# Fox/mLSTM decoder step on one core: the second place of gathered values given up ahead of the seventh MLP step's products, and five stores and one copy at the attention's two ends on other engines

## The chip, the core and the metric

The kernel runs on one core of one Trainium2 chip. The core has TensorE (PE, matrix products), VectorE (DVE), ScalarE (ACT), GpSimd (POOL) and SyncE (SP), which run beside each other and wait for each other by semaphores, and 16 DMA engines, which SP, ACT and POOL start. The metric is the device time of one launch in microseconds (us), the median of several runs; less is better.

## The reference

One step of a decoder layer. A prompt of 2048 tokens and 8 sequences of 8 new tokens (each with 8192 cached positions in pages) go through one input projection, two kinds of heads, one output projection with layer norm, and a squared-ReLU MLP with layer norm. Cut to the prompt's part:

```python
z = x @ w_in                       # fox q, k, v, f; mLSTM q/k, v, i, f, o
# 8 heads of 64: causal attention with forget gates
s = q_i @ k.T * Dh ** -0.5 + L_i[..., :, None] - L[:, :, None, :]
fox = softmax(where(k_pos <= q_pos, s, -inf)) @ v
# 4 heads of 128: matrix memory, chunk by chunk
C_new = g_state * C + einsum('bhs,bshd,bshe->bhde', w_key, k, v)
n_new = g_state * n + einsum('bhs,bshd->bhd', w_key, k)
mix = concat([fox, norm(h) * mlstm_norm_w * sigmoid(o)]) @ w_o
x1  = layer_norm(DN_ALPHA * x + mix)
y   = layer_norm(DN_ALPHA * x1 + square(relu(x1 @ w1)) @ w2)
```

The samples' fox heads attend to `cache_k` and `cache_v` by the page table. C and n after the last chunk are outputs (`C_prompt`, `n_prompt`), as are k and v (`k_prompt`, `v_prompt`).

## The kernel before

Four stages follow one another. The first (0 to 869.5 us) makes the input projections and the matrix memory; the second (to 1309.5, `phase_b`) is the prompt's attention; the third (to 1540, `phase_o`) the output projection and the first layer norm; the fourth (`phase_c`) the MLP. Products in float32 are made of parts: an operand x is split into a rounded part xh (`split_hi`, L153, on ACT) and the rest xl (`split_lo`, L156, on DVE), and `mm3` (L162 to L164) adds three products wh·xh, wl·xh and wh·xl in this order of lines.

Beside all of it the samples' attention runs as a generator, from which the stages take a step now and then. It gathers pages of `cache_v` by POOL's indirect DMAs (L1838) into one of two places: `vt`, which is always there, and a second one, `vx["more"]`, which is lent by the stage that runs and taken back by setting it to `None`. Their products are sO (L1862).

In the attention, `units` lists 64 pairs (head h, block g of 256 queries). `scores` (L981, L982) multiplies the queries' parts qh and ql by the keys' ks, and DVE adds the forget values nl (L989; for the diagonal block nd, which POOL makes of nl and a mask at L974) and takes the maximum. `values` makes the softmax on ACT (L1010), transposes S by TensorE to pt (L1026), copies it to PT (L1029, L1031), multiplies by the values vn to po (L1036), copies one half of po to ot (L1041) and adds the other (L1043). After every fourth block `finish` turns the sums to a row of factors through DRAM (drl, rl), multiplies on POOL (L1061) and stores to `dmix` (L1062). The first head loads nl (L932), vn (L933), the keys kn (L938) and the queries qn (L956) as it goes; the first kn and qn were loaded earlier (L226). `phase_o` loads `dmix` as xr, splits it to mh and ml and multiplies it with the parts of w_o (wh, wl) to pw.

The matrix memory ends with the stores of C (L749) and n (L752, its copy nn), and `turn_out` transposes the last chunk's output (L644, mm), copies it (L646, ot) and stores it to `dmix` (L647).

The code order is the order of creation; a scheduler then fixes each engine's order when the kernel is built. Eight semaphores (DMAHW0 to 7) are given in turn to the DMAs which SP and ACT start, eight others (DMASW0 to 7) to POOL's. A DMA waits until the one that had its semaphore before has landed; each engine takes its instructions strictly in order, so what stands behind such a wait waits too.

Of the kernel before, what the change touches and what calls it, by code (L numbers as in the profile page):

```python
# [25 lines left out]
S = 2048  # L26
# [26 lines left out]
def body(ctx, tc, I, O, stages):  # L53
    nc = tc.nc
    V, A, G, T, SY = nc.vector, nc.scalar, nc.gpsimd, nc.tensor, nc.sync
# [12 lines left out]
    dmix = drm.tile([8, 128, TOT], F32, name="dmix")  # L68
# [40 lines left out]
    vx = dict(more=None, live=[], next=0, of={})  # L109
# [512 lines left out]
    dmv = dmix.rearrange("j p t -> p j t")  # L622
# [3 lines left out]
    def norm_out(hh, np_, og, tok0, eng=None):  # L626

        st = pm.tile([128, 4, 6], F32, name="st6", bufs=2)
        mv = pm.tile([128, 4, 2], F32, name="mv2", bufs=2)
        for h in range(4):  # L630
            V.bn_stats(st[:np_, h], hh[:, h])
            V.bn_aggr(mv[:np_, h], st[:np_, h])
        r = pm.tile([128, 2, 4], F32, name="r4", bufs=2)
        V.tensor_scalar(r[:np_, 0], mv[:np_, :, 1], EPS, None, op0=OP.add)
        G.tensor_tensor(r[:np_, 1], r[:np_, 0], nhalf[:np_, 0:4], op=OP.pow)
        for h in range(4):
            V.tensor_scalar(hh[:, h], hh[:, h], mv[:np_, h, 0:1], r[:np_, 1, h:h + 1], op0=OP.subtract, op1=OP.mult)
        hf = hh.rearrange("p h e -> p (h e)")
        (eng or G).tensor_tensor(hf, hf, og, op=OP.mult)

        def turn():
            po = ppm.tile([128, 4, 128], F32, name="mm", tag="mm", bufs=2)
            for h in range(4):
                T.transpose(po[:, h, :np_], hh[:, h], ident[:np_, :np_])  # L644
            ot = pm.tile([128, 4, 128], F32, name="ot", bufs=1)
            A.copy(ot[:, :, :np_], po[:, :, :np_])  # L646
            SY.dma_start(dmv[:, 4:8, tok0:tok0 + np_], ot[:, :, :np_])  # L647
        mst["turn"] = turn

    def turn_out():  # L650
# [28 lines left out]
    def m_block(bi):  # L679
# [10 lines left out]
        for c in range(bi * 4, bi * 4 + 4):  # L690
            Cs = mst["C"]
# [30 lines left out]
            for p in range(2):  # L722
                yield 1
                pn = ppm.tile([128, 2, 129], F32, name="mn", tag="mm", bufs=2)
                for i in range(2):
                    h = 2 * p + i
# [5 lines left out]
            for p in range(2):  # L732
# [4 lines left out]
                for i in range(2):  # L737
                    h = 2 * p + i
# [7 lines left out]
        if bi < 3:  # L746
            return
        Cs = mst["C"]
        SY.dma_start(O["C_prompt"][0, 0].rearrange("h d e -> d h e"), Cs[:, :, 0:128])  # L749
        nn = pm.tile([128, 4], F32, name="nn", tag="sm", bufs=1)  # L750
        V.tensor_copy(nn, Cs[:, :, 128])
        SY.dma_start(O["n_prompt"], nn)  # L752
        yield 1
        turn_out()

# [148 lines left out]
    def phase_b():  # L904
# [95 lines left out]
        def values(z, g, sc):  # L1000
# [37 lines left out]
            if g % 4 == 0:  # L1038
                z["ot"] = pb.tile([64, 1024], F32, name="ot", bufs=2)
            od = z["ot"][:, (g % 4) * 256:(g % 4) * 256 + 256]  # L1040
            A.copy(od, po[0:64])  # L1041
            q0 = 128 if g == 0 else 0
            V.tensor_tensor(od[:, q0:], od[:, q0:], po[64:128, q0:], op=OP.add)  # L1043
            if g % 4 == 3:
# [2 lines left out]
        def finish(z, half):  # L1047

            h, ls, ot = z["h"], z["ls"], z["ot"]
            lr = pb.tile([128, 32], F32, name="lr", bufs=2)  # L1050
            V.reciprocal(lr, ls)
            lt = pb.tile([128, 32], F32, name="lt", bufs=2)
            V.transpose(lt, lr)
            o = half * 1024
            for a in range(4):
                SY.dma_start(drl[h, o:o + 1024].rearrange("(t a q) -> a t q", a=4, q=32)[a], lt[a * 32 + half * 8:a * 32 + half * 8 + 8])
            for q in range(2):
                rl = pb.tile([64, 512], F32, name="rl", bufs=2)
                SY.dma_start(rl, dap(drl, h * S + o + q * 512, [[0, 64], [1, 512]]))
                s = slice(q * 512, (q + 1) * 512)  # L1060
                G.tensor_tensor(ot[:, s], ot[:, s], rl, op=OP.mult)  # L1061
                SY.dma_start(dmix[h // 2, (h % 2) * 64:(h % 2) * 64 + 64, o + q * 512:o + q * 512 + 512], ot[:, s])  # L1062

        kns = [pb.tile([128, 512], F32, name="kn", bufs=3)]
        homes = {}
# [224 lines left out]
    def phase_c():  # L1290
# [51 lines left out]
        for ci, blk in enumerate(CB):  # L1342
# [201 lines left out]
            hidden(0, 1)  # L1544
            for p in range(8):
                pre = []
                if p == 7 and ci == 3:
                    plain(p)
                    break
                if p < 7:  # L1550
                    hidden(p + 1, 0, lambda: pre.append(ahead(p, *order[:2])))
                else:
                    pre.append(ahead(p, *order[:2]))
                if p == 6:
                    vx["more"] = None
                with ExitStack() as es_:
                    if "normed" in C:
                        es_.enter_context(tc.issue_after(C.pop("normed").ins))
                    output(p, pre[0], begun if p == 7 and ci < 3 else None)
                if p == 7 and ci < 3:  # L1560
                    vx["more"] = landing
                    C["w1"] = w1_pieces(0)
                    C["gb"] = vecs(2)
                    later = [normed(t, ys[t], C["gb"]) for t in blk]
                if p == 6 and ci < 3:
                    take_back()
                    begun = [x1_load(t) for t in CB[ci + 1][:2]]
                if p == 6 and ci == 2:
                    while acc[1] is not None:
                        tick(100.0)  # L1570
                if p < 7:
                    hidden(p + 1, 1, {2: sampled, 3: early}.get(ci) if p == 6 else None)
# [437 lines left out]
```

## Time and profile before

| | us |
|---|---|
| three runs | 3205.98, 3209.95, 3212.35 (median 3209.95) |
| profiled execution | 3212.34 (span 3210.6) |
| granted TensorE clock, mean of the span | 0.989 |
| TensorE busy, 0 to 869.5 | 847.87 of 869.5 |
| TensorE busy, 1309.5 to 1540 | 224.41 of 230.5 |

Times in the profile run from the span's start. In a timeline row the first number is when a group of instructions starts, the second how long it takes, then engine, line, operation, out<-in, shapes and count; brackets hold the idle time of the engine just before it and what ended it. SPq, ACTq and POOLq rows are an engine's DMA issues, and their time is that of issuing, not of the transfer. Ends of matrix products are modelled, so neighbours can overlap a little.

### The profile page before, as it was taken

The page shows a single profiled execution, that of the slowest core. Times are in us where ns is not written, and L with a number is a line of the kernel's source. Part 1 is how long each engine was busy: PE and PEld are TensorE (multiplying, and loading weights), DVE is VectorE, ACT ScalarE, POOL GpSimd, SP SyncE. Part 2 cuts the span into 40 slices and gives each one's busy share as a digit, 9 for nine tenths or more (in the row PEclk, how much of TensorE's full clock was granted, in tenths as well). Part 3 has the DMA queues.
Part 4 walks back from the last instruction along what each step waited for, and adds up shares of the span by engine and source line. Part 5 has one row for each costly group of instructions (what it writes and reads, how often), then busy time and mean ns, then how long its engine had stood idle before and what let it go on. Part 6 is the DMA issues. An engine that isn't in the chain of part 4 may idle for free. (4 is left out here: it accounts for less than half of the span.)

```text
span 3210.6 us, 55049 instructions
## 1 busy us (share of the span) xinstructions
PE 3115.6 (97%) x20445; PEld 2475.3 (77%) x20445; DVE 2080.9 (65%) x5046; ACT 1442.2 (45%) x2654; POOL 902.6 (28%) x973
## 2 busy tenths in 40 slices
PE   8999999999899999999999999999999999899998
PEld 8997797888767667777677777777767777698886
DVE  6957556465488788534557568556675665766667
ACT  3343343333277777412444445343444444344442
POOL 0121223423333333376333323334333111000000
PEclk9999999999999999999999999999999999999999
DMA  5565766866777865687887869878879866643231
GB/s 190 156 216 179 253 210 211 295 238 228 238 241 189 204 170 138 223 295 257 300 289 269 308 234 322 319 260 307 292 260 340 288 209 204 211 165 131 98 126 63
DMA packets 325075, 732.67 MB, mean 228 GB/s; under 512 B 63592, under 2 KB 161384, under 8 KB 323912
## 3 DMA queue, kind: packets, MB, share of 16 engines
q1 hardware_dynamic: 237672, 414.67, 39.8%
q0 software_dynamic: 83520, 304.12, 27.3%
q10 hardware_dynamic: 3616, 10.36, 0.9%
q8 instruction: 162, 2.65, 0.3%
q14 instruction: 105, 0.86, 0.1%
HBM read 676.20 MB, written 86.38 MB: 238 GB/s over the span
## 5 line engine op out<-in xcount | busy, mean ns | idle before, releaser
L156 DVE TENSOR_TENSOR wl<-wr,wh 128x1024 fp32r<-128x1024 f32 x300 | 365.9, 1223 | 244.0 <-ACT wh L153 204.8
L153 ACT ACTIVATE wh<-wr 128x1024 fp32r<-128x1024 f32 x300 | 315.3, 1055 | 332.0 <-PE py L164 123.7
L162 PE MATMUL ph<-x1h,wh 128*128 128x512 f32 (+1 forms) x1280 | 455.4, 356 | 0.0
L163 PE MATMUL ph<-x1l,wh 128*128 128x512 f32 (+1 forms) x1280 | 453.7, 355 | 0.2 <-DVE x1l L156 0.2
L164 PE MATMUL ph<-x1h,wl 128*128 128x512 f32 (+1 forms) x1280 | 451.7, 355 | 0.2
L1727 POOL DMA_INDIRECT kT<-cache_k,idxK x256 | 277.0, 1082 | 551.9 <-PE sQ L1750 483.2
L162 PE MATMUL py<-wh,hh 128*128 128x512 f32 x900 | 358.9, 403 | 10.1 <-issue 3.6
L163 PE MATMUL py<-wl,hh 128*128 128x512 f32 x900 | 354.5, 395 | 0.2 <-issue 0.2
L164 PE MATMUL py<-wh,hl 128*128 128x512 f32 x900 | 351.8, 395 | 0.4 <-DVE hl L156 0.4
L1376 DVE TENSOR_TENSOR y<-y,py 128x512 f32<-128x512 f32 x410 | 277.2, 683 | 108.4 <-PE py L164 83.0
L1838 POOL DMA_INDIRECT vt<-cache_v,idxV x164 | 178.9, 1091 | 401.4 <-PE sO L1862 341.5
L162 PEld LDWEIGHTS ph<-x1h,wh 128*128 128x128 f32 x1280 | 241.4, 189 | 40.6 <-issue 8.2
L164 PEld LDWEIGHTS ph<-x1h,wl 128*128 128x128 f32 x1280 | 240.8, 189 | 36.5 <-issue 3.7
L163 PEld LDWEIGHTS ph<-x1l,wh 128*128 128x128 f32 x1280 | 241.5, 189 | 34.9 <-issue 3.7
L162 PE MATMUL pm<-whi,xh 128*128 128x256 f32 (+2 forms) x816 | 238.2, 292 | 8.0 <-ACT whi L153 7.9
L163 PE MATMUL pm<-wlo,xh 128*128 128x256 f32 (+2 forms) x816 | 233.9, 287 | 1.0 <-DVE wlo L156 0.6
L164 PE MATMUL pm<-whi,xl 128*128 128x256 f32 (+2 forms) x816 | 234.1, 287 | 0.0
L162 PE MATMUL pm<-xh,whi 128*128 128x512 f32 (+2 forms) x640 | 230.5, 360 | 0.0
L164 PE MATMUL pm<-xh,wlo 128*128 128x512 f32 (+2 forms) x640 | 227.4, 355 | 0.0
L163 PE MATMUL pm<-xl,whi 128*128 128x512 f32 (+2 forms) x640 | 226.8, 354 | 0.0
L162 PEld LDWEIGHTS py<-wh,hh 128*128 128x128 f32 x900 | 169.3, 189 | 66.1 <-issue 25.8
L164 PEld LDWEIGHTS py<-wh,hl 128*128 128x128 f32 x900 | 170.7, 190 | 40.3 <-issue 2.3
(364 smaller groups left out, 6545.2 us busy)
## 6 DMA issues: line engine op xcount, KB each, us to landing
wr<-w SPq DMA_DIRECT2D x200, 512.0 KB
wra<-w_in SPq DMA_DIRECT2D x104, 512.0 KB
wr<-dw SPq DMA_DIRECT2D x96, 512.0 KB
dw<-w POOLq DMA_DIRECT2D x48, 512.0 KB
Rb<-dR SPq DMA_DIRECT2D x128, 128.0 KB
kT<-dw SPq DMA_DIRECT2D x28, 512.0 KB
kT<-w SPq DMA_DIRECT2D x25, 512.0 KB
xn<-xp_t SPq DMA_DIRECT2D x16, 512.0 KB
```

Of the source, the lines that this page charges most:

```text
L153: last["ACT"] = A.activation(dst, src, AF.Copy, scale=scale)
L156: r = (eng or V).tensor_tensor(dst, src, hi.bitcast(F32), op=OP.subtract)
L162: T.matmul(ps, wh, xh, start=first, stop=False, skip_group_check=shared)
L163: T.matmul(ps, wh, xl, start=False, stop=False, skip_group_check=shared)
L164: last["PE"] = T.matmul(ps, wl, xh, start=False, stop=stop, skip_group_check=shared)
L1376: V.tensor_tensor(y, y, ps, op=op)
L1727: G.indirect_dma_start(out=piece(n), out_offset=None, in_=ck, in_offset=IO(ap=idxK[:, b, j // 2, j % 2:j % 2 + 1], axis=0))
L1838: vx["last"] = G.indirect_dma_start(out=vt.rearrange("p f c -> p (f c)"), out_offset=None, in_=cv, in_offset=IO(ap=idxV[:, b, (kt % 4) * 4 ...
```

## The change

The stores of C_prompt, n_prompt and the last mLSTM chunk's output are started by ACT instead of SP. At the attention's end, the last unit's copy of po is made by DVE instead of ACT, and the last two stores to `dmix` are started by POOL instead of SP. In the MLP, `vx["more"] = None` at p == 6 is set before the call of `hidden(7, 0)` instead of after it. Lines behind L1041 have a number higher by 3 in the changed kernel. `turn_out`, `finish` and `values` are called as before.

```diff
--- before.py
+++ after.py
@@ -644,7 +644,7 @@
                 T.transpose(po[:, h, :np_], hh[:, h], ident[:np_, :np_])
             ot = pm.tile([128, 4, 128], F32, name="ot", bufs=1)
             A.copy(ot[:, :, :np_], po[:, :, :np_])
-            SY.dma_start(dmv[:, 4:8, tok0:tok0 + np_], ot[:, :, :np_])
+            (A if tok0 == S - 128 else SY).dma_start(dmv[:, 4:8, tok0:tok0 + np_], ot[:, :, :np_])
         mst["turn"] = turn
 
     def turn_out():
@@ -746,10 +746,10 @@
         if bi < 3:
             return
         Cs = mst["C"]
-        SY.dma_start(O["C_prompt"][0, 0].rearrange("h d e -> d h e"), Cs[:, :, 0:128])
+        A.dma_start(O["C_prompt"][0, 0].rearrange("h d e -> d h e"), Cs[:, :, 0:128])
         nn = pm.tile([128, 4], F32, name="nn", tag="sm", bufs=1)
         V.tensor_copy(nn, Cs[:, :, 128])
-        SY.dma_start(O["n_prompt"], nn)
+        A.dma_start(O["n_prompt"], nn)
         yield 1
         turn_out()
 
@@ -1038,7 +1038,10 @@
             if g % 4 == 0:
                 z["ot"] = pb.tile([64, 1024], F32, name="ot", bufs=2)
             od = z["ot"][:, (g % 4) * 256:(g % 4) * 256 + 256]
-            A.copy(od, po[0:64])
+            if (z["h"], g) == units[-1]:
+                V.tensor_copy(od, po[0:64])
+            else:
+                A.copy(od, po[0:64])
             q0 = 128 if g == 0 else 0
             V.tensor_tensor(od[:, q0:], od[:, q0:], po[64:128, q0:], op=OP.add)
             if g % 4 == 3:
@@ -1059,7 +1062,7 @@
                 SY.dma_start(rl, dap(drl, h * S + o + q * 512, [[0, 64], [1, 512]]))
                 s = slice(q * 512, (q + 1) * 512)
                 G.tensor_tensor(ot[:, s], ot[:, s], rl, op=OP.mult)
-                SY.dma_start(dmix[h // 2, (h % 2) * 64:(h % 2) * 64 + 64, o + q * 512:o + q * 512 + 512], ot[:, s])
+                (G if (h, half) == (7, 1) else SY).dma_start(dmix[h // 2, (h % 2) * 64:(h % 2) * 64 + 64, o + q * 512:o + q * 512 + 512], ot[:, s])
 
         kns = [pb.tile([128, 512], F32, name="kn", bufs=3)]
         homes = {}
@@ -1544,6 +1547,8 @@
             hidden(0, 1)
             for p in range(8):
                 pre = []
+                if p == 6:
+                    vx["more"] = None
                 if p == 7 and ci == 3:
                     plain(p)
                     break
@@ -1551,8 +1556,6 @@
                     hidden(p + 1, 0, lambda: pre.append(ahead(p, *order[:2])))
                 else:
                     pre.append(ahead(p, *order[:2]))
-                if p == 6:
-                    vx["more"] = None
                 with ExitStack() as es_:
                     if "normed" in C:
                         es_.enter_context(tc.issue_after(C.pop("normed").ins))
```

How the instructions stand, at three places. First SP at the attention's start, from the last Rb loads of the samples' attention to the first queries. The bracket names the semaphore whose former DMA has to have landed (DMAHW), or the engine waited for. Before:

```order
L1734 DMA Rb<-dR 128x1x256 [waits DMAHW5_49]
L749 DMA C_prompt<-Cs 128x4x128 [waits DMAHW7_49,DVE_49]
L752 DMA n_prompt<-nn 128x4 [waits DMAHW0_49,DVE_49]
L647 DMA dmix<-ot 128x4x128 [waits DMAHW1_49,Activation_49]
L932 DMA nl_10000<-dnl 128x512 [waits DMAHW2_49]
L933 DMA vn_9999<-v_prompt 128x4x64 [waits DMAHW3_49]
L938 DMA kn<-k_prompt 64x512 [waits DMAHW4_49]
L938 DMA kn<-k_prompt 64x512 [waits DMAHW5_49]
L932 DMA nl_10000<-dnl 128x512 [waits DMAHW6_49]
L933 DMA vn_9999<-v_prompt 128x4x64 [waits DMAHW7_49]
L956 DMA qn<-dq 64x256 [waits DMAHW0_49,PE_49]
```

Now, SP and then ACT:

```order
L1737 DMA Rb<-dR 128x1x256 [waits DMAHW5_49]
L932 DMA nl_10000<-dnl 128x512 [waits DMAHW1_49]
L933 DMA vn_9999<-v_prompt 128x4x64 [waits DMAHW3_49]
L938 DMA kn<-k_prompt 64x512 [waits DMAHW4_49]
L938 DMA kn<-k_prompt 64x512 [waits DMAHW5_49]
L932 DMA nl_10000<-dnl 128x512 [waits DMAHW6_49]
L933 DMA vn_9999<-v_prompt 128x4x64 [waits DMAHW7_49]
L956 DMA qn<-dq 64x256 [waits DMAHW0_49,PE_49]
```

```order
L604 DMA v_prompt<-st 128x256 [waits DMAHW6_49,Activation_49]
L749 DMA C_prompt<-Cs 128x4x128 [waits DMAHW7_49,DVE_49]
L752 DMA n_prompt<-nn 128x4 [waits DMAHW0_49,DVE_49]
L646 COPY ot<-mm 128x512 [waits DMAHW1_49,PE_49]
L153 ACTIVATE qh<-qn_9739 128x256 [waits DMAHW5_49]
L153 ACTIVATE ks_10001<-kn_9738 128x512
L647 DMA dmix<-ot 128x4x128 [waits DMAHW2_49,Activation_49]
L1010 ACTIVATE S,lp<-S,mx 128x128 [waits DVE_49]
```

The first nl is no longer behind the three stores. The second nl, the vn behind it and the first qn wait on DMAHW6, 7 and 0, and the DMAs which had these before them are v_prompt, C_prompt and n_prompt, in both kernels; in the changed one they are in ACT's queue.

Second, TensorE at the same time: the first unit of the attention. Before:

```order
L644 MATMUL mm<-ident,hh 128x128 x4
L981 MATMUL pS<-ks_10001,qh 128x256
L982 MATMUL pS<-ks_10001,ql 128x256
L981 MATMUL pS<-ks_10001,qh 128x256
L982 MATMUL pS<-ks_10001,ql 128x256
L1026 MATMUL pt<-ident,S 128x128 x3
L981 MATMUL pS<-ks_10001,qh 128x384
L981 MATMUL pS<-ks_10001,qh 128x512
L1036 MATMUL po<-PT,vn_9999 64x256
L1036 MATMUL po<-PT,vn_9999 64x128
L982 MATMUL pS<-ks_10001,ql 128x384
```

Now:

```order
L1026 MATMUL pt<-ident,S 128x128 x3
L1036 MATMUL po<-PT,vn_9999 64x256
L1036 MATMUL po<-PT,vn_9999 64x128
L981 MATMUL pS<-ks_10001,qh 128x384
L981 MATMUL pS<-ks_10001,qh 128x512
L982 MATMUL pS<-ks_10001,ql 128x384
```

The first unit's po products stand ahead of the second unit's first scores. A few products and transposes of the next units of the first head changed places in the same way; from there on TensorE's order is the same to the end.

Third, the attention's end: ACT before, with the last unit's copy ahead of the output projection's splits, and DVE now.

```order
L1041 COPY ot<-po 64x256
L1029 COPY PT<-pt 128x4x128 x3
L1029 COPY PT<-pt 128x3x128
L1029 COPY PT<-pt 128x4x128
L1041 COPY ot<-po 64x256
L153 ACTIVATE mh<-xr 128x1024
L153 ACTIVATE wh<-wr 128x1024 x4
```

```order
L1031 COPY PT<-pt 128x4x128
L1042 COPY ot<-po 64x256
L1046 TENSOR_TENSOR ot<-ot,po 64x256
L84 MEMSET pad_5x 128x1
L156 TENSOR_TENSOR ml<-xr,mh 128x1024
L156 TENSOR_TENSOR wl<-wr,wh 128x1024 x4
```

The second copy of ot has left ACT, where mh and wh now follow the copies of PT, and stands on DVE between a copy of PT and the addition. Everything behind stands as before.

## The prediction

> **What bounds the kernel now.** I read the page first, then busy time by stage, then TensorE's waits, and only then the two places which the diff touches, engine by engine. From the page:
>
> ```profile
> span 3210.6 us, 55049 instructions
> PE 3115.6 (97%) x20445; PEld 2475.3 (77%) x20445; DVE 2080.9 (65%) x5046; ACT 1442.2 (45%) x2654; POOL 902.6 (28%) x973
> ```
>
> TensorE (PE) is busy for 3115.6 of 3210.6 us, so 95.0 us of idle time is all that an edit which leaves its work alone can win. By stage (columns: stretch, its length, then busy time of PE, PEld, DVE, ACT, POOL, the granted PE clock, DMA share, GB/s):
>
> ```profile
> 869.50:1309.50 440.00, 416.33 (x2880) 295.80 (x2880) 348.88 (x1373) 327.95 (x765) 151.74 (x237) 0.98 0.68 180
> 1540.00:3210.60 1670.60, 1626.95 (x9869) 1263.97 (x9867) 1089.19 (x1838) 727.81 (x1123) 380.85 (x365) 0.99 0.68 238
> ```
>
> The attention leaves 23.7 us idle, the MLP 43.7 us. TensorE's waits, by what they wait for (total, times, longest):
>
> ```profile
> PE sO L1862 <- DMA vt<-cache_v,idxV: 18.3, 6, 6.2
> PE pt L1026 <- ACT S L1010: 10.5, 3, 7.4
> ```
>
> The first is the waiting for gathered values, which the MLP edit is about. The second contains one stall of 7.4 us, and it stands exactly where the stores are moved, at the attention's start:
>
> ```profile
> 869.54 0.58 PE L981 MATMUL pS<-ks,qh 128*128 128x256 f32 x1 [2.23 <-DVE ks L156]
> ...
> 870.35 0.41 PE L982 MATMUL pS<-ks,ql 128*128 128x256 f32 x1
> 878.18 0.48 PE L1026 MATMUL pt<-ident,S 128*128 128x128 f32 x1 [7.42 <-ACT S L1010]
> ...
> 879.65 1.11 PE L981 MATMUL pS<-ks,qh 128*128 128x384 f32 x2
> 880.70 1.12 PE L1036 MATMUL po<-PT,vn 128*64 128x256 f32 x4
> 881.74 1.12 PE L982 MATMUL pS<-ks,ql 128*128 128x384 f32 x2
> ```
>
> Four score products end at 870.76 (878.18 less 7.42). Then TensorE waits for the first softmax. What that softmax waits for is seen on GpSimd (POOL) and on SyncE's queue:
>
> ```profile
> 876.53 1.69 POOL L974 TENSOR_TENSOR nd<-nl,dmask 128x128 f32<-128x128 f32 x4 [8.70 <-DMA nl<-dnl]
> ```
>
> ```profile
> 862.69 1.18 SPq L1734 DMA_DIRECT2D Rb<-dR  x2
> 867.14 0.39 SPq L749 DMA_DIRECT2D C_prompt<-Cs  x1
> 867.62 0.72 SPq L752 DMA_DIRECT2D n_prompt<-nn  x1
> 868.43 0.63 SPq L647 DMA_DIRECT2D dmix<-ot  x1
> 869.12 0.68 SPq L932 DMA_DIRECT2D nl<-dnl  x1
> ...
> 870.38 1.25 SPq L938 DMA_DIRECT2D kn<-k_prompt  x2
> 874.23 0.34 SPq L932 DMA_DIRECT2D nl<-dnl  x1
> 874.76 0.37 SPq L933 DMA_DIRECT2D vn<-v_prompt  x1
> 875.23 2.38 SPq L956 DMA_DIRECT2D qn<-dq  x4
> ```
>
> The forget values nl leave SP at 869.12, behind three stores, and are used at 876.53. SP then stands still until 874.23, and only afterwards come the next queries (875.23). Why it stands:
>
> ```profile
> SPq L932 <- DMA v_prompt<-st: 2.6, 1, 2.6
> SPq L933 <- DMA C_prompt<-Cs: 0.2, 1, 0.2
> ```
>
> Eight semaphores are handed out in turn to the DMAs of SP and ACT, so a load waits for the store that had its semaphore eight DMAs ago. The second nl waits for a v_prompt store, the vn behind it for C_prompt.
>
> **The change, part by part: the attention's start.** The stores of C_prompt, n_prompt and the last dmix go to ScalarE's (ACT) queue. SP can issue the first nl when the Rb pair is out, at 862.69 + 1.18 = 863.87, instead of 869.12: 5.25 us earlier. By the trip that it has now (869.12 to 876.53, 7.41 us) its use would be at about 871.3, and the first unit of attention (softmax, transposes pt, products po) would run in what is now idle time.
>
> The second step is the next unit's queries. Their loads stand behind the second nl and vn, and by the instruction rows of the changed kernel these still wait for the same stores: nl for v_prompt, vn for C_prompt, qn for n_prompt. None of them leaves earlier than now:
>
> ```profile
> 865.94 0.34 ACTq L604 DMA_DIRECT2D v_prompt<-st  x1
> 879.19 0.96 ACT L153 ACTIVATE qh<-qn 128x256 fp32r<-128x256 f32 x2
> ```
>
> v_prompt is issued by ACT at 865.94, before and after the change, and C_prompt can't go ahead of 867.14, when its data is ready. So if the landings stay, qn leaves at 875.23 as now, and the second unit's scores stay near 879.65. Most of the stall is then only split up, not removed. Two things remain. The first unit's po products now stand ahead of these scores, where before they stood behind the first two of them: 881.74 less 880.70, 1.04 us, moves into the idle time. And the queries' trip, 875.23 to 879.19, is 3.96 us now, with the first nl, vn and kn still under way. A load at the attention's end takes less:
>
> ```profile
> 1304.27 1.11 SPq L1059 DMA_DIRECT2D rl<-drl  x2
> 1307.28 1.26 POOL L1061 TENSOR_TENSOR ot<-ot,rl 64x512 f32<-64x512 f32 x1 [23.25 <-DMA rl<-drl]
> ```
>
> That is 3.01 us, 0.95 less. Together 2.0 us, which I take. The bounds are 5.25 us of gain (everything from the first nl on moves with it) and a loss of 7.4 us (the stores land later by the whole trip of the load that now goes ahead of them). I take a value near nothing because the rows name v_prompt and C_prompt, and neither is issued earlier.
>
> On ACT the two issues stand ahead of the ot copy and of the splits qh and ks: 0.39 + 0.72 = 1.11 us later first scores. Queued behind them is everything of ACT; TensorE waits for it, but its scores would end at 871.9 and nl is due at 871.3, so this costs nothing as long as the softmax waits for loads. If that cover goes, it costs 1.11 us. The third store's issue (0.63 us) lies in ACT's wait for the softmax.
>
> The scheduler also put some products and transposes of the next units in another order. The nearest row for what such a place can cost is
>
> ```profile
> 905.12 0.66 PE L1026 MATMUL pt<-ident,S 128*128 128x128 f32 x4 [2.59 <-ACT S L1010]
> ```
>
> so it lies between -2.6 (this wait vanishes) and +2.6 us (one more like it). I take 0, as the same work is done and no row favours a side.
>
> **The attention's end.** There one copy goes from ACT to VectorE (DVE), and two stores from SP to POOL:
>
> ```profile
> 1305.88 3.67 PE L1036 MATMUL po<-PT,vn 128*64 128x256 f32 x32
> 1311.92 0.50 PE L162 MATMUL pw<-wh,mh 128*128 128x512 f32 x1 [2.38 <-ACT wh L153]
> 1314.05 0.80 PE L163 MATMUL pw<-wl,mh 128*128 128x512 f32 x1 [1.62 <-DVE wl L156]
> ```
>
> ```profile
> 1309.60 0.37 ACT L1041 COPY ot<-po 64x256 f32<-64x256 f32 x1 [3.03 <-PE po L1036]
> ```
>
> ```profile
> 1310.00 0.42 DVE L1043 TENSOR_TENSOR ot<-ot,po 64x256 f32<-64x256 f32 x1 [4.30 <-ACT ot L1041]
> 1310.96 1.90 DVE L156 TENSOR_TENSOR ml<-xr,mh 128x1024 fp32r<-128x1024 f32 x1 [0.53 <-ACT mh L153]
> ```
>
> Now ACT waits 3.03 us for the last po before it may begin the output projection's splits mh and wh. Without the copy they run ahead, and the 2.38 us wait for wh goes. But the next product needs wl, which DVE makes after ml, and DVE still has copy and add first. By ACT's 0.37 the copy would end at 1309.97 and the add at 1310.39; ml starts near 1310.45 instead of 1310.96, and wl and the product at 1314.05 move with it: 0.5 us. The 2.38 us becomes a longer wait at the second product. The bounds are 1.0 us of gain (the hand-off and the short memset both hidden) and 0.4 us of loss (a copy twice as long as ACT's).
>
> On POOL a store's issue costs
>
> ```profile
> L1140 POOL DMA_DIRECT2D dw<-w x48 | 35.5, 793 | 0.1
> ```
>
> 0.79 us, so two delay what is behind them, the gathers of vx, by 1.6 us. Their first use on TensorE is
>
> ```profile
> 1341.63 1.05 PE L1862 MATMUL sO<-vx,PTs 128*32 128x256 f32 x16
> ```
>
> some 30 us after the stage's start, so I cost this at nothing; with that cover gone it would be 1.6 us. SP is relieved of the same two, but its next loads still wait for POOL's last product.
>
> **The MLP.** The two lines which move one assignment ahead of a call change no row: every engine has the same instructions in the same order, with the same waits, and each wait has the same producer. So no gather is issued between the old place of the assignment and the new one. I take 0.
>
> **The sum** is -2.0 - 0.5 = -2.5 us. The profiled execution took 3212.34 us, its span 3210.6 and 1.74 around it, so it would take 3209.8. It lies 2.39 us above the median of the three runs shown, 3209.95, so against the median the forecast is 3207.4 us.
>
> **The rivals.**
>
> First, the whole train moves (B). If v_prompt and C_prompt land sooner, as fewer loads are issued in one burst with them, the later loads follow the first, and the stall shrinks by 5.25 us. The clock then gains as well:
>
> ```profile
> 872.00:880.00 8.00, 1.29 (x4) 0.82 (x5) 2.14 (x12) 2.25 (x8) 2.14 (x5) 0.50 0.83 204
> 880.00:890.00 10.00, 9.02 (x43) 5.55 (x42) 8.64 (x41) 5.61 (x14) 2.92 (x5) 0.84 0.81 230
> ```
>
> In the stall it is 0.50, in the ten microseconds behind it 0.84. With no such stall that is 1.6 us. 5.25 + 1.6 + 0.5 = 7.35, giving 3202.6 us. For it: from 867.14 to 871.63 SP issues three stores and the loads nl and kn in one burst. Against it: a v_prompt that leaves at 865.94 needed until 874.23 with little issued just behind it.
>
> Second, nothing comes of the start (C). In 880 to 890 DVE is busy for 8.64 of 10 us, so what TensorE wins ahead of it DVE may take back: only the end's 0.5 stays, 3209.4 us. The Trainium skill speaks for this outcome: "DMA: Bandwidth & Descriptors", section "Issuing engines are not separate DMA queues", says that transfers started by different engines run interleaved on the same 16 DMA engines, and that spreading them saves only the sequencer's time to start them. By that rule the three stores would save SP's issue time alone, 0.39 + 0.72 + 0.63 = 1.74 us. The trace bears it out so far as SP's wait of 2.6 us is for a store that ACT had issued; it does not speak of what stands behind a waiting store, which is the 5.25 us here.
>
> Third, slower (D): the moved loads delay the stores. The first nl and vn now go out ahead of C_prompt and n_prompt, and share the DMA engines (busy share 0.83) with them. If C_prompt lands later by the trip of such a load, 7.4 us, then the second vn, and behind it the queries, leave at 882.6, and TensorE stands until then: 7.4 - 0.5 = 6.9 us slower, 3216.8 us. It decides from the point where C_prompt lands after 874.76. For it: all of them move through the same engines. Against it: the loads would be done sooner, too, and leave the engines free.
>
> Fourth, the MLP edit does what its words say (E): one wait for gathered values of up to 6.2 us goes, 3207.4 - 6.2 = 3201.2 us. Against it stand the identical rows.
>
> **How the numbers follow.** A has 0.40, B 0.32, C 0.13, D 0.13, E 0.02. A measurement of this kernel tells about 0.2%, 6.4 us, from no change (its three runs lie within that), so the bounds are 3203.5 and 3216.4. With a scatter of some 3 us, A gives faster, same, slower 0.14, 0.80, 0.06 of its chance, B 0.65, 0.35, 0, C 0.03, 0.87, 0.10, D 0, 0.30, 0.70, and E is faster. Faster: 0.056 + 0.208 + 0.004 + 0.02 = 0.29. Same: 0.320 + 0.112 + 0.113 + 0.039 = 0.58. Slower: 0.024 + 0.013 + 0.091 = 0.13. A's own range is 3204.5 to 3210.5 (the scheduler's 2.6 either way and the end's bounds). The whole range takes in B with its scatter and C, and leaves out most of D: 3199.5 to 3213.5 us.
>
> **What would show it.** In the new profile nl's first load should leave SP near 863.9 and be used near 871; the second nl should still wait for v_prompt until about 874, and the second scores start near 878. If they start below 875, B holds; above 881, D. At the end wh and mh should run before 1309.6, with DVE's copy and add ahead of ml. The waits for vt in the MLP should be within what two executions differ by. A wait of the vx products would show the cost on POOL. The forecast is wrong if the landing of v_prompt or C_prompt moves by more than about 2 us, since the landings carry it.

## The result, and the profile after

| | median of 20 runs, us | profiled execution, us (span) | granted clock |
|---|---|---|---|
| before | 3206.74 | 3212.34 (3210.6) | 0.989 |
| changed | 3217.28 | 3217.23 (3215.5) | 0.986 |

The changed kernel takes 1.0033 times as long, with a 95% interval of 1.0023 to 1.0042: 10.5 us slower by the medians. The profiled executions differ by only 4.9 us, because the one of before lies 5.6 us above its median (the median of the three runs shown at first, 3209.95, was 3.2 us above it) and the one of the change lies at its median. So the loss has to be looked for by place, not by the difference of the two spans.

The page and TensorE's waits over the whole span, of the changed kernel:

```profile
span 3215.5 us, 55049 instructions
PE 3116.5 (97%) x20445; PEld 2478.0 (77%) x20445; DVE 2084.4 (65%) x5047; ACT 1443.9 (45%) x2653; POOL 912.5 (28%) x975
```

```profile
PE sO L1865 <- DMA vt<-cache_v,idxV: 17.8, 9, 5.9
...
PE pw L162 <- ACT woh L153: 5.1, 1, 5.1
...
PE pw L163 <- DVE wl L156: 2.8, 1, 2.8
```

The work is the same. The waits for gathered values are too (18.3 before). New is a wait of 5.1 us for woh, the split of the second half of w_o: it stands some 25 us behind the attention's end, where the prediction had no term. The timeline shows where it comes from. VectorE and GpSimd at the attention's end:

```profile
1315.57 0.42 DVE L1042 COPY ot<-po 64x256 f32<-64x256 f32 x1 [3.90 <-PE po L1036]
1316.02 0.42 DVE L1046 TENSOR_TENSOR ot<-ot,po 64x256 f32<-64x256 f32 x1
1316.37 1.22 DVE L156 TENSOR_TENSOR ml<-xr,mh 128x1024 fp32r<-128x1024 f32 x1
...
1317.51 4.62 DVE L156 TENSOR_TENSOR wl<-wr,wh 128x1024 fp32r<-128x1024 f32 x4
1322.05 1.21 DVE L156 TENSOR_TENSOR ml<-xr,mh 128x1024 fp32r<-128x1024 f32 x1
1323.19 1.21 DVE L156 TENSOR_TENSOR wol<-wr,woh 128x1024 fp32r<-128x1024 f32 x1
```

```profile
1313.58 1.29 POOL L1064 TENSOR_TENSOR ot<-ot,rl 64x512 f32<-64x512 f32 x1 [23.59 <-DMA rl<-drl]
1315.16 0.59 POOL L1065 DMA_DIRECT2D dmix<-ot  x1 [0.30 <-POOL ot L1064]
1316.52 9.02 POOL L1064 TENSOR_TENSOR ot<-ot,rl 64x512 f32<-64x512 f32 x1 [0.77 <-DVE pad_5x L84]
1325.84 0.56 POOL L1065 DMA_DIRECT2D dmix<-ot  x1 [0.30 <-POOL ot L1064]
```

GpSimd's last multiplication took 9.02 us; the one before it took 1.29. It begins at 1316.52, 0.15 us behind VectorE's first split ml, and ends at 1325.54, 1.14 us behind the last of VectorE's unbroken row of splits (1323.19 + 1.21 = 1324.40). Before the change the same operation came first:

```profile
1310.50 1.27 POOL L1061 TENSOR_TENSOR ot<-ot,rl 64x512 f32<-64x512 f32 x1 [1.96 <-DVE pad_5x L84]
```

There ml started 0.46 us later, at 1310.96, and took 1.90 us. The next ml of that row took 1.21:

```profile
1317.32 1.21 DVE L156 TENSOR_TENSOR ml<-xr,mh 128x1024 fp32r<-128x1024 f32 x1
```

So the two already stood in each other's way before the change, with GpSimd in front and VectorE losing 0.7 us.

What waits for the multiplication is SyncE's queue. SyncE in the changed kernel, its wait, and the two engines at the end of the chain:

```profile
1311.43 15.95 SPq L1230 DMA_DIRECT2D y<-x_prompt  x5
1327.42 0.71 SPq L1203 DMA_DIRECT2D xr<-dmix  x1
1328.18 5.45 SPq L1148 DMA_DIRECT2D wr<-w_o  x3
```

```profile
SPq L1230 <- POOL ot L1064: 11.5, 1, 11.5
```

```profile
1339.45 1.06 ACT L153 ACTIVATE woh<-wr 128x1024 fp32r<-128x1024 f32 x1 [20.28 <-DMA wr<-w_o]
```

```profile
1340.56 0.79 PE L162 MATMUL pw<-woh,mh 128*128 128x512 f32 x1 [5.12 <-ACT woh L153]
```

By the wait row the load of the second y waits for the last multiplication (11.5 us), most likely because it goes into memory which the attention's ot and rl held, and behind it in SyncE's queue stand the loads of w_o. They leave at 1328.18, 12.6 us behind the last unit's copy (1315.57). Before, they left at 1315.88, 6.3 us behind it (1309.60):

```profile
1315.88 6.43 SPq L1145 DMA_DIRECT2D wr<-w_o  x3
```

What was expected of the copy itself came true beside this. The wait for wh is gone, the second product waits 2.83 us where the two waits were 2.38 and 1.62, and starts 6.93 us behind the start of the last po products instead of 8.17 (1318.78 less 1311.85, 1314.05 less 1305.88): 1.2 us won.

At the attention's start the changed kernel's rows are, for TensorE, SyncE and ScalarE:

```profile
864.49 0.66 PE L644 MATMUL mm<-ident,hh 128*128 128x128 f32 x4 [0.25 <-DVE Cs L739]
868.98 0.58 PE L981 MATMUL pS<-ks,qh 128*128 128x256 f32 x1 [3.84 <-DVE ks L156]
...
871.69 0.47 PE L1026 MATMUL pt<-ident,S 128*128 128x128 f32 x1 [1.49 <-ACT S L1010]
875.62 0.69 PE L1026 MATMUL pt<-ident,S 128*128 128x128 f32 x2 [3.45 <-ACT S L1010]
876.87 1.09 PE L1036 MATMUL po<-PT,vn 128*64 128x256 f32 x4 [0.57 <-issue]
879.15 1.11 PE L981 MATMUL pS<-ks,qh 128*128 128x384 f32 x2 [1.20 <-ACT qh L153]
```

```profile
861.76 0.58 SPq L932 DMA_DIRECT2D nl<-dnl  x1
...
874.15 0.33 SPq L932 DMA_DIRECT2D nl<-dnl  x1
```

```profile
863.78 0.34 ACTq L604 DMA_DIRECT2D v_prompt<-st  x1
```

The first nl leaves early, and the first transpose starts 7.2 us behind mm where it was 11.5. The first scores start later, 4.5 us behind mm where it was 2.9 (866.65 to 869.54): ScalarE's two issues, of C_prompt and n_prompt, took 0.70 and 0.91 us, and they stand ahead of its splits. This stays hidden behind the wait for nl. Then the stall returns in pieces. The second nl still waits for the v_prompt store: it leaves 10.4 us behind that store's issue (863.78 to 874.15), where it was 8.3 (865.94 to 874.23). The second unit's scores start 14.7 us behind the transposes mm (864.49 to 879.15). Before, it was 13.0, by the row of mm there:

```profile
866.65 0.66 PE L644 MATMUL mm<-ident,hh 128*128 128x128 f32 x4 [0.25 <-DVE Cs L739]
```

### The profile page after: what moved, and what is told of

It is laid out like the page before. It is cut to its first block, busy times and chain, and to the rows that moved or that the text cites. A ratio compares the mean times of both kernels' runs of the same rounds, so it can differ in the third digit from the quotient of the medians.

```text
span 3215.5 us, 55049 instructions
## 1 busy us (share of the span) xinstructions
PE 3116.5 (97%) x20445; PEld 2478.0 (77%) x20445; DVE 2084.4 (65%) x5047; ACT 1443.9 (45%) x2653; POOL 912.5 (28%) x975
```

## The experiments

Every kernel was timed in five rounds beside the kernel before on the same chip; the ratios are to that. Three things were to be told apart: the copy with GpSimd's multiplication (theory P), the two stores on GpSimd (S), and the attention's start (A). First each part of the change alone.

**The copy alone**

```diff
-            A.copy(od, po[0:64])
+            if (z["h"], g) == units[-1]:
+                V.tensor_copy(od, po[0:64])
+            else:
+                A.copy(od, po[0:64])
```

> The kernel before with the last unit's copy of po made by VectorE as the only edit. Theory P (the last multiplication on GpSimd loses its turn): with the copy gone from ScalarE, VectorE's splits ml, wl follow the addition without a gap, GpSimd's last multiplication of ot by rl takes about 9 us instead of 1.3, SyncE's second load of y waits for it, the w_o loads behind it leave some 10 us later, and the kernel is 5 to 9 us slower (ratio 1.0015 to 1.003). Theory S (the two stores on GpSimd do it): the multiplication stays at 1.3 us and the kernel is 0.5 to 1.2 us faster (ratio 0.9996 to 1.000). Theory A (only the attention's start costs): as S.

Measured: 1.0033 (1.0019 to 1.0047). GpSimd, VectorE and TensorE of this kernel:

```profile
1314.90 9.03 POOL L1064 TENSOR_TENSOR ot<-ot,rl 64x512 f32<-64x512 f32 x1 [1.94 <-DVE pad_5x L84]
```

```profile
1314.76 1.22 DVE L156 TENSOR_TENSOR ml<-xr,mh 128x1024 fp32r<-128x1024 f32 x1
...
1321.57 1.22 DVE L156 TENSOR_TENSOR wol<-wr,woh 128x1024 fp32r<-128x1024 f32 x1
```

```profile
1342.67 0.79 PE L162 MATMUL pw<-woh,mh 128*128 128x512 f32 x1 [10.15 <-ACT woh L153]
```

One moved copy of 0.4 us gives the whole loss. The multiplication starts 0.14 us behind ml, takes 9.03 us and ends 1.14 us behind the last split (1322.79), the same distance as in the changed kernel. The wait for woh is 10.15 us. The dmix store now stands in SyncE's queue as well, and the w_o loads leave 13.9 us behind the copy instead of 12.6; the rest of the longer wait is not explained by that. Theories S and A fall as the cause of the loss.

**The stores on GpSimd alone**

```diff
-                SY.dma_start(dmix[h // 2, ...], ot[:, s])
+                (G if (h, half) == (7, 1) else SY).dma_start(dmix[h // 2, ...], ot[:, s])
```

> The kernel before with the last two stores to dmix on GpSimd's queue as the only edit. Theory P: the multiplication stays at 1.3 us, as VectorE's splits still wait for ScalarE behind its copy; the time stays within 2 us (ratio 0.9995 to 1.0006). Theory S: the last multiplication and with it the loads of w_o come late, 5 to 9 us slower (ratio 1.0015 to 1.003).

Measured: 1.0005 (0.9990 to 1.0020). The multiplication takes 1.26 us, and no product waits for woh. Each store's issue on GpSimd takes 0.59 or 0.56 us, and the gathers behind them are not late for anything.

**The attention's start alone**

```diff
-            SY.dma_start(dmv[:, 4:8, tok0:tok0 + np_], ot[:, :, :np_])
+            (A if tok0 == S - 128 else SY).dma_start(dmv[:, 4:8, tok0:tok0 + np_], ot[:, :, :np_])
...
-        SY.dma_start(O["C_prompt"][0, 0].rearrange("h d e -> d h e"), Cs[:, :, 0:128])
+        A.dma_start(O["C_prompt"][0, 0].rearrange("h d e -> d h e"), Cs[:, :, 0:128])
...
-        SY.dma_start(O["n_prompt"], nn)
+        A.dma_start(O["n_prompt"], nn)
```

> The kernel before with the three stores at the attention's start on ScalarE's queue as the only edit. In the changed kernel's profile TensorE is 3.0 us further behind at the 45th microsecond of the attention than at its start, against the kernel before. If that is the edit's doing: 2 to 4 us slower (ratio 1.0006 to 1.0012), the second unit's scores not before 878 us and a low clock until about 890. If it is the scatter of one execution: within 1 us, or 2 us faster as forecast (ratio 0.9993 to 1.0003).

Measured: 1.0004 (0.9993 to 1.0015). The profile repeats that of the whole change (second unit's scores 14.0 us behind mm), but the interval tells neither 3 us slower (1.0009) nor no change from each other. A gain of 2 us (0.9994) lies just inside it, too, so the time alone does not refute the forecast for this part; the rows do, as the scores come later instead of earlier.

**The MLP's assignment alone**

```diff
                 pre = []
+                if p == 6:
+                    vx["more"] = None
                 if p == 7 and ci == 3:
...
-                if p == 6:
-                    vx["more"] = None
```

> The kernel before with the assignment of the second place moved ahead of the products as the only edit. No instruction row changes, so every theory expects the same time (ratio 1.000, and its distance from 1 shows what the measurement itself does). If the edit did something after all, one wait for gathered values in the MLP would change by up to 6 us (ratio 0.998 to 1.002).

Measured: 1.0001 (0.9988 to 1.0015). No row of any engine differs, so this is what the measurement makes of two equal kernels.

The next three take one link of the chain away each, all with the copy on VectorE.

**A wait that lets GpSimd go first.** Behind the addition VectorE reads one column of what the multiplication wrote:

```diff
                 G.tensor_tensor(ot[:, s], ot[:, s], rl, op=OP.mult)
+                if (h, half, q) == (7, 1, 1):
+                    V.tensor_copy(lr[0:64, 0:1], ot[:, 1023:1024])
```

> As the copy alone, and one more edit: behind the addition VectorE copies one column of ot that GpSimd's last multiplication has written, so that it waits for that multiplication and starts the splits ml, wl only then. The copy's place, the stores and SyncE's order are those of the copy alone. Theory P (GpSimd's operation can't start while VectorE runs operations on two operands in SBUF back to back): the multiplication takes 1.3 us again, the w_o loads leave about when they do before, and the time returns to the kernel before's within 2 us (ratio 0.9994 to 1.0006). Theory Q (the copy itself, or the early splits on ScalarE, make the loads late): it stays 7 to 11 us slower (ratio 1.002 to 1.0035).

Measured: 1.0001 (0.9992 to 1.0010). GpSimd and VectorE:

```profile
1324.80 1.26 POOL L1064 TENSOR_TENSOR ot<-ot,rl 64x512 f32<-64x512 f32 x1 [2.11 <-DVE ot L1046]
```

```profile
1326.09 0.15 DVE L1066 COPY lr<-ot 64x1 f32<-64x1 f32 x1 [1.37 <-POOL ot L1064]
1326.17 1.23 DVE L156 TENSOR_TENSOR ml<-xr,mh 128x1024 fp32r<-128x1024 f32 x1
```

An added wait of 1.37 us on VectorE takes the loss away. The copy, the early splits on ScalarE and SyncE's order are those of the copy alone; only who starts first has changed. Theory Q falls.

**The multiplication on VectorE**

```diff
-                G.tensor_tensor(ot[:, s], ot[:, s], rl, op=OP.mult)
+                (V if (h, half, q) == (7, 1, 1) else G).tensor_tensor(ot[:, s], ot[:, s], rl, op=OP.mult)
```

> As the copy alone, and the last unit's last multiplication of ot by rl made by VectorE instead of GpSimd, behind the addition. Theory P: nothing is left on GpSimd that could be kept out; 0.7 us for the multiplication stands ahead of ml, the hand-offs to ScalarE and GpSimd are gone, 0 to 1 us faster than the kernel before (ratio 0.9993 to 1.0003). Theory Q: it stays 7 to 11 us slower (ratio 1.002 to 1.0035).

Measured: 0.9991 (0.9977 to 1.0006). The multiplication takes 0.68 us there, and the w_o loads leave 6.2 us behind the copy, as before the change.

**The second y out of SyncE's queue.** Copy and both stores as in the change, and:

```diff
-            SY.dma_start(xs[t], x_of(t))
+            (G if t == 1 else SY).dma_start(xs[t], x_of(t))
```

> The copy on VectorE and the two stores on GpSimd, without the attention's start and the MLP; and the load of the second y, for which SyncE waits until GpSimd's last multiplication is done, is started by GpSimd itself. Theory P with its second half (the loss comes through SyncE's queue, where the w_o loads stand behind that y): the multiplication still takes 9 us, but the w_o loads leave 5 to 10 us earlier than with the copy alone, the wait for woh is gone, and the kernel is 0 to 1.5 us faster than before (ratio 0.9993 to 1.0003). Rival R (the late multiplication costs by itself, or the loads are late because their buffers are): 5 to 10 us slower (ratio 1.0015 to 1.003).

Measured: 0.9993 (0.9980 to 1.0006). GpSimd, SyncE and TensorE:

```profile
1314.12 9.03 POOL L1064 TENSOR_TENSOR ot<-ot,rl 64x512 f32<-64x512 f32 x1 [1.19 <-DVE pad_5x L84]
```

```profile
1316.35 2.60 SPq L1148 DMA_DIRECT2D wr<-w_o  x3
```

```profile
1316.38 0.50 PE L163 MATMUL pw<-wl,mh 128*128 128x512 f32 x1 [2.83 <-DVE wl L156]
1335.53 0.50 PE L163 MATMUL pw<-wol,mh 128*128 128x512 f32 x1 [1.00 <-DVE wol L156]
```

The multiplication is as slow as in the change (9.03 us), and it costs next to nothing any more: the w_o loads leave 3.2 us behind the copy (1313.17 in this kernel), and the wait of 5.1 us for woh is gone; the second half of w_o begins with a wait of 1.00 us, for wol. So the slow operation is harmless in itself, and the loss comes through the queue. Rival R falls.

Then the start, and the whole.

**The second queries ahead of the second keys.** The start alone, and in the attention's loop:

```diff
+                if n == 0:
+                    queries(Z[0], 1)
                 if h == 0 and g % 2 == 0 and g < 6:
                     keys(Z[0], g // 2 + 1)
...
-                if n + 1 < len(units):
+                if n and n + 1 < len(units):
                     queries(Z[units[n + 1][0]], units[n + 1][1])
```

> The three stores of the attention's start on ScalarE's queue, as in the change, and the second unit's queries are loaded ahead of the second block of keys, so that they take the semaphores of the Rb loads instead of those of the stores C_prompt and n_prompt. Theory V (the stores' landings hold the queries): the second unit's scores start some 5 us earlier than in the start alone, the half-speed clock of about 24 us gets shorter, and the kernel is 3 to 7 us faster than the start alone (ratio to the kernel before 0.998 to 0.9996). Rival W (the stall only moves, to the second block of keys, and the clock stays low): ratio 0.9997 to 1.001.

Measured: 1.0014 (1.0004 to 1.0024), slower than before. The second unit's scores do start earlier, 10.2 us behind mm, but the keys now have the semaphores of the stores and leave 10.2 us behind v_prompt's issue (868.75 to 878.90), and TensorE waits for them a little further on. The stall moved, as rival W had it, and theory V falls. The price is a little above W's range, which ended at 1.001.

**The whole change with the multiplication on VectorE**, the edit of e6 in the changed kernel:

> The whole change with one more edit: the last unit's last multiplication on VectorE. Theory P as the cause of nearly all of the loss: what is left is the attention's start, within 2.5 us of the kernel before (ratio 0.9995 to 1.0008). If the start or the stores carry a share of their own: 3 to 7 us slower (ratio 1.001 to 1.002).

Measured: 0.9998 (0.9984 to 1.0013). With this one operation moved, the whole loss is gone. Since e9 and the change differ in nothing else, their rows show where it arises. From the first wol product to the next sQ, TensorE has the same products to do. In the change, and then in e9:

```profile
1333.99 0.50 PE L163 MATMUL pw<-wol,mh 128*128 128x512 f32 x1
1352.40 1.93 PE L1753 MATMUL sQ<-kT,qb 128*32 128x256 f32 x32
```

```profile
1331.14 0.50 PE L163 MATMUL pw<-wol,mh 128*128 128x512 f32 x1
1341.83 1.93 PE L1753 MATMUL sQ<-kT,qb 128*32 128x256 f32 x32
```

That is 18.41 us against 10.69. Before, it was 10.69 too (1329.19 to 1339.88), and with the copy alone (e1) 23.98 (1331.08 to 1355.06). The windows show what the 7.7 us consist of. The change, from the second product on, and e9 at the same places (columns as in the prediction's windows: length, PE, PEld, DVE, ACT, POOL, granted clock, DMA share, GB/s):

```profile
1318.00:1328.00 10.00, 9.22 (x28) 7.35 (x29) 6.40 (x6) 1.17 (x2) 9.17 (x3) 0.66 0.14 32
...
1340.50:1347.00 6.50, 6.44 (x18) 5.11 (x19) 4.27 (x4) 2.12 (x3) 0.00 (x0) 0.62 1.06 403
```

```profile
1317.00:1327.00 10.00, 9.80 (x36) 7.94 (x37) 7.53 (x9) 1.43 (x2) 7.72 (x2) 0.83 1.04 401
...
1332.40:1339.00 6.60, 6.60 (x30) 5.45 (x29) 0.00 (x1) 0.23 (x1) 1.42 (x2) 1.00 1.05 415
```

While SyncE stands still, the DMA engines move 32 GB/s instead of 401. TensorE, for want of weights, waits 5.1 us, and behind the wait its clock is lower: 0.62 against 1.00 in 6.5 us is 2.5 us of work. Together 7.6 us, next to the 7.7. The lower clock of the first window, 0.66 against 0.83, lies ahead of the wait and can't come from the loads: from the second product to the first wol the change took 15.21 us (1318.78 to 1333.99) and e9 13.94 (1317.20 to 1331.14), but the kernel before, with its loads on time, took 15.14 (1314.05 to 1329.19).

So by place the end costs 7.7 us and wins 1.2 at the second product, 6.5 us in all. The medians say 10.5 us (7.4 to 13.5 by the interval), and where the rest arises is not shown: single executions scatter by as much. TensorE's way from mm to the last po products took 439.2 us before and 447.4 in the change, but 438.0 in e1 and 448.7 in e5, whose start is as before.

**The end alone in its best form**: copy and last multiplication on VectorE, the two stores on GpSimd, the start and the MLP as before.

> The kernel before with the end alone: the last copy and the last multiplication on VectorE, the last two stores on GpSimd. By theory P and the earlier runs (copy with multiplication 0.9991, stores alone 1.0005): 0 to 4 us faster than before (ratio 0.9988 to 1.000). If a store between GpSimd's gathers costs by itself: 1 to 3 us slower (ratio 1.0003 to 1.001).

Measured: 0.9992 (0.9979 to 1.0006). The three kernels with a mended end (e6, e7, e10) lie 0.7 to 0.9 thousandths below the kernel before, each with an interval that holds 1: they clearly beat the change, but that they beat the kernel before isn't shown.

**Two of the three stores of the start, and the third.** C_prompt and n_prompt on ScalarE's queue, with the dmix store left on SyncE's:

> The kernel before with C_prompt and n_prompt alone on ScalarE's queue; the first nl is then ahead of the dmix store, vn and the keys behind it. Theory G (the early nl breaks one stall into several, and the half-speed clock lasts longer): the half-speed stretch behind the attention's start is again longer than 13.7 us (17 to 24), and the time within 3 us of the kernel before, not faster (ratio 1.000 to 1.001). Rival (ScalarE's issues do it): the stretch stays at 13.7 us and the scores start 1 us later, with a ratio of 1.000 to 1.0004.

and the other way round:

> The kernel before with the last chunk's dmix store alone on ScalarE's queue; nl stays behind C_prompt and n_prompt and leaves some 0.7 us earlier. Theory G: one stall of 6.5 to 7.5 us as before, a half-speed stretch of 13.7 us (10 to 14), and the same time (ratio 0.9995 to 1.0004). Rival: as in the other half.

Measured: 1.0003 (0.9990 to 1.0016) and 1.0006 (0.9994 to 1.0019). Busy times in the stretch from 15 to 25 us behind mm, for the kernel before, the change, e9, e11 and e12 (columns as in the prediction's windows; the granted clock is the third figure from the end):

```profile
881.65:891.65 10.00, 8.49 (x45) 5.85 (x44) 9.23 (x46) 6.81 (x16) 3.37 (x6) 0.93 0.79 216
```

```profile
879.49:889.49 10.00, 8.37 (x23) 5.50 (x23) 6.51 (x32) 4.54 (x12) 2.33 (x4) 0.50 0.81 221
```

```profile
880.65:890.65 10.00, 8.91 (x44) 6.15 (x43) 9.05 (x45) 6.10 (x15) 2.42 (x6) 0.80 0.82 226
```

```profile
881.64:891.64 10.00, 9.17 (x29) 6.84 (x28) 7.71 (x38) 4.66 (x12) 2.79 (x5) 0.50 0.84 247
```

```profile
877.25:887.25 10.00, 8.31 (x48) 5.67 (x48) 9.51 (x47) 7.40 (x17) 3.36 (x6) 0.93 0.87 250
```

With the dmix store alone moved there is one stall of 6.14 us and a clock of 0.93, as before; with the other two moved the first nl goes out early, the stall is in pieces, and the clock is 0.50. That fits theory G: half speed lasted some 21 us in e11 and 14 in e12, as it expected of each. But the change's own start, with like pieces, had 0.50 twice (the change and e3) and 0.80 once (e9), and e8's pieces had 0.77, so a broken stall makes the low clock likely, not sure. Where the stall was whole (before, e1, e2, e4 to e7, e10, e12) it was 0.78 to 0.96.

| kernel | copy to w_o loads, us | last multiplication, us | second scores behind mm, us | ratio |
|---|---|---|---|---|
| before | 6.3 | 1.27 | 13.0 | 1 |
| change | 12.6 | 9.02 | 14.7 | 1.0033 |
| e1 copy | 13.9 | 9.03 | 12.4 | 1.0033 |
| e2 stores on GpSimd | 4.9 | 1.26 | 12.6 | 1.0005 |
| e5 copy, GpSimd first | 6.0 | 1.26 | 12.4 | 1.0001 |
| e6 copy, multiplication on VectorE | 6.2 | 0.68 (DVE) | 12.8 | 0.9991 |
| e7 copy, y on GpSimd | 3.2 | 9.03 | 12.5 | 0.9993 |
| e9 change, multiplication on VectorE | 4.1 | 0.68 (DVE) | 14.5 | 0.9998 |
| e10 end alone, mended | 4.1 | 0.68 (DVE) | 12.4 | 0.9992 |

The ratio is above 1.002 only where the w_o loads leave more than 12 us behind the copy, and they do so only where the multiplication is slow and SyncE waits for it.

## Why the prediction was wrong, point by point

**The attention's end** was forecast at -0.5 us, and it is where the loss is. The step that failed is the sentence "its next loads still wait for POOL's last product", costed at nothing with GpSimd's 1.27 us taken as fixed. The runs show it at 9.0 us whenever VectorE's splits start ahead of it, by 0.14 or 0.15 us (the change, e1, e7), and in the change, with the w_o loads behind it in SyncE's queue, that cost 5.1 us of waiting and 2.5 us of clock. A row for a warning was in the prediction: ml at 1.90 us, against 1.21 of its like, right behind an addition after which GpSimd and VectorE are both released. Moving the copy took away the 0.53 us in which VectorE waited for ScalarE's mh; I counted that as a hand-off saved, and it was the gap in which GpSimd got in. What the prediction said of the splits themselves was right in kind (wh early, the second product the new wait) and too small (1.2 us in place of 0.5, slightly above its bound of 1.0).

The Trainium skill has the rule, and it speaks against this change: "SBUF — State Buffer", section "Who interferes with whom", says that a VectorE instruction with two inputs in SBUF (the memory on the core) and a GpSimd instruction that reads SBUF exclude each other for a whole instruction, that the one issued first has the way and that the other is held up entirely. The trace agrees on the order (GpSimd first: 1.27 us, and ml 1.90; VectorE first: 9.02) and goes further: seven such instructions of VectorE without a gap held GpSimd up for all of them, not for one. Its end came 1.14, 1.14 and 1.15 us behind the last of the row in the change, e1 and e7.

**The attention's start** was forecast at -2.0 us. Its two conditions were named rightly, that the second nl and the queries still wait for the stores, and the first nl's gain came as worked out in kind (the first transpose 4.3 us earlier behind mm). What failed is "if the landings stay": from the v_prompt store to the second nl it went from 8.3 to 10.4 us in the change, 10.1 in e3, 10.4 in e9 and 8.9 in e11, while it was 7.4 to 8.0 in the other kernels in which the first nl is issued behind that store. The prediction had named a move of more than about 2 us there as a sign of being wrong. It fits rival D's mechanism, at 2 us instead of its 7.4; the second scores at 879.15 lie ahead of D's mark of 881, but mm is 2.2 us earlier in this execution, so counted from mm they are at it. The two gains of the term came in part: the po products moved into the idle time (876.87), and the queries' trip shortened from 3.96 us to 3.62 (875.06 to 878.68) instead of 3.01. But the queries left 2.0 us later behind mm, and the second scores came 0.9 to 1.7 us later instead of 2.0 earlier. In time it is 1.0004 (0.9993 to 1.0015), in which nothing and a gain of 2 us both lie.

**The stores on GpSimd** at nothing: 1.0005 (0.9990 to 1.0020), in line; an issue took 0.56 to 0.59 us where the row of other stores gave 0.79. The sign named for a cost there, a wait of the vx products, does appear in the change: 1.9 us at 1519.57. It stands some 190 us behind the two stores, though, and it was 2.5 us in e6 and 0.7 in e4, which leave these stores on SyncE, and none in e2, which moves them, so it is not theirs. **The MLP** at nothing: 1.0001, in line. **The scheduler's new order** at nothing: the same work as in e3, not told apart from the start.

**The rivals.** The likeliest case and B lie on the wrong side. D, with 0.13, gave 3216.8 us, next to the 3217.3 measured, but by another mechanism: what it priced at 7.4 us was worth 2, and the loss came from the attention's end, with a mechanism that no rival spoke of. That the number fits is chance. The range ended at 3213.5, below the result, because it held no bound for a slower operation on GpSimd: apart from the copy's and the queries' trip, its bounds moved start times about and took the durations as fixed.

## What to carry to other kernels

When an edit closes a gap on VectorE, look up what GpSimd runs at that moment: an operation on GpSimd that reads SBUF and becomes ready just behind a row of two-operand operations on VectorE can wait for the whole row, and a duration in the profile that is above its like, here by 0.7 us, can be the sign that the two already meet. Then ask what stands in a queue behind the one that waits: here 8 us on an engine off the path cost TensorE 7.7 us only because SyncE's next weights stood behind a load that waited for it, and starting that one load from GpSimd, or multiplying on VectorE, took the cost away. Where a load was moved ahead of a store on another queue, the store landed later: the next load that waits for it left 7.4 to 8.3 us behind the store's issue with nl behind the store, 8.9 with nl ahead of it (e11), and 10.1 to 10.4 with nl and vn ahead. That the loads and the store share the DMA engines is the likely reason; no run separates it.

## What the hardware showed that I had not expected

GpSimd's gather, too, can be longer under such a row: with the multiplication gone from GpSimd, the first gather of vx behind it took 7.72 us in e10 and 7.73 in e9, against 1.09 where it ran ahead of the row in e6. But under the row it also took 1.87 us before, 1.99 in e2 and 2.13 in e5, so the row alone does not do it, and the condition stays open. It cost nothing here, as vx is used later.

TensorE's half-speed clock behind the attention's start lasted, in three of five kernels (the change, e3 and e11, not e8 and e9), for the whole stretch from 15 to 25 us behind mm after a stall in pieces (1.5, 3.5, 0.6, 1.2 and 0.7 us in the change). After one whole stall (7.42 us before, 6.14 in e12) a mean clock of 0.93 there leaves it 1.4 us of the stretch: less idle time in a row went with more time at the low clock. The Trainium skill, "TensorE: Matmul & The Clock Gate", section "What's actually happening", ties the return to full speed to one sustained busy window of about 3.4 us; the pieces could deny it one. The trace agrees in part only: inside the stretch the change's longest wait was 0.66 us, e9 had 0.80 behind the same pieces, and no run here shows which pieces count.
